# Low halves of four weight tiles computed by POOL instead of DVE, and a new planned price of the transposes

## The chip, the cores and the metric

The kernel runs on one core of a Trainium2 chip. The metric is the device time of one execution in microseconds, the median of several runs. Five engines work side by side: PE (matrix multiplication, with its weight load PEld), DVE (vector), ACT (scalar and activation), POOL (general purpose), and SP, whose queue issues the DMA transfers here.

## The reference

A causal decoder trunk of two layers, for one sequence of 256 tokens of width 1024, all in float32:

```
h = x
for i in range(2):
    mix = moba_attention(h, ...)      if i == 0     # 16 heads of 64
          dilated_attention(h, ...)   if i == 1     # 12 heads of 64, three windows
    h = layer_norm(alpha * h + mix)
    h = layer_norm(alpha * h + square(relu(h @ w_in)) @ w_out)   # 1024 -> 4096 -> 1024
```

Both attentions project to q, k and v, apply rotary embedding to q and k, take a softmax over masked scores, and project back with an output matrix. In the second layer the three groups of four heads have windows 128, 512 and 2048 with steps of 1, 4 and 16, and the groups' results are weighted by their softmax denominators, which comes to one softmax over the three groups together.

## The kernel before

**Numbers in two parts.** To multiply in nearly full float32, every operand is split into a high part, rounded to the matmul's float32r type, and a low part, the difference. A product is then three matmuls: high by high, low by high and high by low. `split` makes the two parts: ACT writes the high one with a copy that rounds (line 337), DVE writes the low one with a subtraction (line 342). For weights, `load_w` takes a `raw` buffer (5 of them, 128x1024 float32, 512 KB), loads a tile into it over SP's queue, and splits it into `whi` and `wlo` (`NSLOT`, 9 of each). 180 tiles of 128x1024 pass this way in one execution.

**Order of the work.** Nothing is issued as it is written. Each step is recorded by `op` with its engine, an assumed duration, and what it reads and writes. `Plan.order` then goes through the steps twice. The first pass runs PE's steps in the order of the program with their assumed durations and gives every step a due time, the latest at which what depends on it is still in time. The second is a list scheduler: for each engine, of the steps that can start first, the one with the earliest due time is taken (DVE may wait a little for a more urgent one). Loads keep their order. The result is a fixed order of instructions for each engine, and the hardware keeps to it, with waits where one engine needs another's result. So an assumed duration is never executed, but changes the order.

**The second layer's attention** follows the string `ORDER1`: three projections `qk-0`, `qk-1`, `qk-2`, each of four weight tiles of 128 output columns, with scores and softmax (`s`), the value projection (`v`), and two output steps (`o`) in between. A projection, `mm_wide`, first multiplies all four tiles' high parts (32 matmuls of 512 columns, the two parts of the input beside each other) and then the four tiles' low parts in order (8 matmuls of 256 columns each). `rotate` applies the rotary embedding on DVE and splits the result into `rhi` and `rlo`, which `score` multiplies. `turned` transposes the softmax result `e` on PE in blocks of 32 columns, 12 blocks to a group of heads in layer 0 and 16 in layer 1, and copies it out as `pt`, two of four parts by DVE and two by ACT in layer 1. Its assumed duration is `0.2 + TURN * len(blocks)`. `pv_dilated` multiplies `pt` by the values and splits the result into `ahi` and `alo`. The output projection reads six weight tiles (`wo1`), the first three for the first output step, the others for the second, each with two token halves and two column halves (`mm_rows`). Then `ln_half` does the LayerNorm: DVE for sums and scaling, POOL for one power instruction of one element per partition (line 756).

**POOL before** does that power instruction eight times, one more at the start, and four small fills. The duration that the planner assumes for elementwise work on POOL is n/480 + 0.17 us for n elements (`tt`), against n/960 + 0.07 on DVE.

Of the kernel before, what the change touches and what calls it, by code (L numbers as in the profile page):

```python
# [10 lines left out]
ALU = mybir.AluOpType  # L11
# [17 lines left out]
NX = (1, 1)  # L29
TAIL = (5, 5, 6, 7)  # L30
NSLOT = 9
TURN = 0.06
DVE1 = (1, 3)
ORDER0 = "qk-0 v-0 qk-1 s-0 o-0 qk-2 s-1 x-0 x-1 o-1 qk-3 s-2 g-0 v-1 s-3 o-2 b-0 o-3"
HEAD1 = "00"
# [54 lines left out]
class Plan:  # L90
# [16 lines left out]
    def op(self, eng, cost, fn, reads=(), writes=(), xfer=0.0, early=0.0, ahead=0.0):  # L107
        o = Op()
        o.n, o.eng, o.cost, o.fn, o.xfer = len(self.ops), eng, cost, fn, xfer
        o.early, o.ahead = early, ahead  # L110
        o.preds, o.succs, o.bufs = set(), [], set()
        for group, is_write in ((reads, False), (writes, True)):
            for item in group:
                b, key = item if isinstance(item, tuple) else (item, None)
                o.bufs.add(b)
                for k, st in b.state.items():
                    if key is None or k is None or k == key:
                        if st[0] is not None:
                            o.preds.add(st[0])
                        if is_write:  # L120
                            o.preds.update(st[1])
                st = b.state.setdefault(key, [None, []])
                if is_write:
                    if key is None:
                        b.state = {None: [o, []]}
                    else:
                        st[0], st[1] = o, []
                else:
                    st[1].append(o)
        o.preds.discard(o)  # L130
        for p in o.preds:
            p.succs.append(o)
        for b in o.bufs:
            b.left += 1
        self.ops.append(o)
        return o
# [141 lines left out]
def tile_trunk(  # L278
# [22 lines left out]
    nc = tc.nc  # L301
    plan = Plan()
    op = plan.op
# [12 lines left out]
    def mk(shape, dt, tag, bufs, space=None):  # L316
        uid[0] += 1
        return plan.buf(Bufs(space or sb, bufs), shape, dt, tag, bufs, f"{tag}_{uid[0]}")

    def psum(tag):  # L320
        return mk([P, 512], F32, tag, 4, ps_pool)

    def f32(ap):
        return ap.bitcast(F32)

    def act(n, aps=0, sbuf=False):
        return n / 1200 + (0.093 if sbuf else 0.055) + 0.093 * aps

    def dve(n, aps=0, fast=False):
        return n / (1920 if fast else 960) + 0.07 + 0.06 * aps  # L330

    def dma(dst, src, reads=(), writes=(), nbytes=0):
        op("SP", ISSUE, lambda: nc.sync.dma_start(dst(), src), reads, writes, xfer=nbytes)  # L333

    def split(n, src, hi, lo, r, whi, wlo, sbuf=False, hi_eng="ACT"):
        if hi_eng == "ACT":
            op("ACT", act(n, sbuf=sbuf), lambda: nc.scalar.activation(hi(), src(), AF.Copy), r, whi)  # L337
        else:
            op("DVE", dve(n), lambda: nc.vector.tensor_copy(hi(), src()), r, whi)
        op(  # L340
            "DVE", dve(n),
            lambda: nc.vector.tensor_tensor(lo(), src(), f32(hi()), op=ALU.subtract), list(r) + list(whi), wlo,  # L342
        )

    def mm(out_ap, lhsT, rhs, start, stop):
# [2 lines left out]
    class W:  # L348
        pass

    def load_w(src, n=1024):
        w = W()
        w.raw = mk([P, 1024], F32, "raw", 5)
        w.hi = mk([P, 1024], F32R, "whi", NSLOT)
        w.lo = mk([P, 1024], F32R, "wlo", NSLOT)
        dma(lambda: w.raw.t[:, :n], src[:, :n], (), [(w.raw, 0)], P * n * 4)
        split(
            n, lambda: w.raw.t[:, :n], lambda: w.hi.t[:, :n], lambda: w.lo.t[:, :n],
            [(w.raw, 0)], [(w.hi, 0)], [(w.lo, 0)], sbuf=True,
        )  # L360
        return w

# [84 lines left out]
    ropes = [const(rope0, [P, 2, S], "ropet")]  # L447
# [127 lines left out]
    def proj_qk(ws):  # L575
        pss = [psum("acc") for _ in ws]
        mm_wide(pss, ws)
        return pss
# [59 lines left out]
    def turned(blocks, r, on_dve=()):  # L638
# [9 lines left out]

        op("PE", 0.2 + TURN * len(blocks), go, list(r) + [ident], pss)
        pt = mk([P, 16, P], F32, "pt", 1)  # L650
# [177 lines left out]
    class Mlp:  # L828
# [3 lines left out]

        def head(self):
            i, nx = self.i, self.nx
            self.ws = [[load_w(win[i][c * 4 + j]) for j in range(4)] for c in range(nx)]
            self.chunks = {c: act_tiles() for c in range(nx)}
            self.half(0)

# [135 lines left out]
    def layer1(between):  # L974
        m1 = late["m1"]
        attn = [act_tiles() for _ in range(2)]

        quads = (((0, 0), (0, 1)), ((0, 2), (1, 0)), ((1, 1), (1, 2)))
        qk, units, seen = {}, {}, [None, None]
        for step, a in (x.split("-") for x in ORDER1.split()):  # L980
            if step == "v":
                v1(int(a[0]), int(a[1]))
                continue
            n = int(a)
            if step == "qk":
                qk[n] = rotate(proj_qk([load_w(wqk1[4 * n + i]) for i in range(4)]), ropes[1])
            elif step == "gb":
                gb = load_gb(2)
            elif step == "s":
                blocks, pss = [], []  # L990
                for u, gi in quads[n]:
                    if u not in units:
                        units[u] = (
                            [[mk([P, 512], F32, "e", 8) for _ in range(2)] for m in range(2)],
                            mk([P, NG, 4], F32, "mx3", 2),
                            mk([P, 8], F32, "sm", 4),
                        )
                    for h in range(2):
                        pss.append(psum("tp"))
                        if gi == 0:  # L1000
                            blocks.append([(halves[m], slice(0, S), m * S) for m in range(2)])
                        else:
                            blocks.append([(halves[m], halves[m], m * P) for m in range(2)])
                score(pss, qk.pop(n), blocks)
                for i, (u, gi) in enumerate(quads[n]):
                    e, st, sm = units[u]
                    w, c0 = (S, 0) if gi == 0 else (P, P + gi * P)
                    g0, seen[u] = seen[u], gi
                    for h in range(2):
                        ps = pss[2 * i + h]  # L1010
                        for m in range(2):
                            r = 2 * h + m
                            mask_min(
                                w, lambda t=e[m][h], c0=c0, w=w: t.t[:, c0 : c0 + w],
                                lambda ps=ps, m=m, w=w: ps.t[:, m * w : (m + 1) * w],
                                lambda m=m, c0=c0, w=w: m1.t[:, m, c0 : c0 + w],
                                lambda st=st, g0=g0, r=r: BIG if g0 is None else st.t[:, g0, r : r + 1],
                                lambda st=st, gi=gi, r=r: st.t[:, gi, r : r + 1],
                                [ps, m1] + ([(st, (g0, r))] if g0 is not None else []), [(e[m][h], gi), (st, (gi, r))],
                            )  # L1020
                    if (n, i) in ((1, 0), (2, 1)):
                        regs = [(e[m][h], 2 * h + m) for h in range(2) for m in range(2)]
                        for t, r in regs:
                            exps(
                                512, lambda t=t: t.t, lambda st=st, r=r, gi=gi: st.t[:, gi, r : r + 1],
                                lambda sm=sm, r=r: sm.t[:, r : r + 1], [t, (st, (gi, r))], [t, (sm, r)],
                            )
                        for t, r in regs:
                            recip(lambda sm=sm, r=r: sm.t[:, r : r + 1], [(sm, r)])
                            scale_by(512, lambda t=t: t.t, lambda sm=sm, r=r: sm.t[:, r : r + 1], [t, (sm, r)], [t])  # L1030
            else:
                e, st, sm = units[n]
                vs, vcs = [], []
                for gi in range(NG):
                    pair = n * NG + gi
                    vs.append(V1[0] if pair < 4 else V1[1])
                    vcs.append(pair * P if pair < 4 else (pair - 4) * P)
                pv_dilated(e, vs, vcs, *attn[n], AHEAD1[n])
        items = [((*attn[j // 3], j % 3), load_w(wo1[j]), j, 6) for j in range(6)]
        out_and_ln(new_acc(), items, TAIL[2], gb, False, between)  # L1040

    mlps = [Mlp(0, False), Mlp(1, True)]
# [119 lines left out]
```

## Time and profile before

| | |
|---|---|
| median of 3 runs | 561.92 us (561.68 to 562.03) |
| profiled execution | 562.14 us, of which the span of instructions 560.3 us |
| granted clock of PE, mean | 0.996 |
| PE busy | 550.7 us (98% of the span), 3459 matmuls |
| DVE busy | 409.9 us (73%) |
| ACT busy | 297.0 us (53%) |
| POOL busy | 8.4 us (1%), 13 instructions |
| DMA | 105.63 MB, mean 189 GB/s |

A row of the timeline or of a group has the engine, the line of the kernel, the operation, `output<-inputs` by tile names, and the shape. Timeline rows begin with start and length in us; a row with x4 is four such instructions in a run, and the bracket at its end tells of idle time before it and of what ended that. In a row of groups, behind the bar, stand the total busy us and the mean ns of one instruction, then the idle us before them and what ended it. Neighbouring instructions of one engine overlap a little in the records, so 4 subtractions of 1.22 us each fill 4.6 us.

### The profile page before, as it was taken

To read this page: it belongs to the slowest core of one execution; us is meant where nothing else is said; L and a number is where in the kernel's file an instruction comes from. 1 tells how busy PE (TensorE), PEld (TensorE's weight loads), DVE (VectorE), ACT (ScalarE), POOL (GpSimd) and SP (SyncE) were. 2 spreads that over 40 slices of the span, in tenths; PEclk is the share of its full clock that TensorE was granted. 3 is DMA by queue.
4 is the path that set the end of the run, shared out by engine and by line. 5 is a ranking of instruction groups with operands and counts; after the bars stand their busy time and mean duration, and the time that the engine had idled before them with its cause. 6 is when DMAs were issued, how large, how long until landed. Compare 5 with 4: busy or idle time off the path is not lost.

```text
span 560.3 us, 8977 instructions
## 1 busy us (share of the span) xinstructions
PE 550.7 (98%) x3459; PEld 467.8 (83%) x3459; DVE 409.9 (73%) x733; ACT 297.0 (53%) x495; POOL 8.4 (1%) x13
## 2 busy tenths in 40 slices
PE   8999999999999999999999999999999999999994
PEld 7888887778888888888888888878888888888884
DVE  6879999797673853855777999998847548557465
ACT  6768866557463555444534547555644554445400
POOL 0000000000000000000000000010000000000000
PEclk9999999999999999999999999999999999999998
DMA  8992345628856755656534742545849566466001
GB/s 309 351 345 81 123 148 178 232 87 318 253 181 269 254 163 185 224 154 223 159 116 156 240 135 101 165 174 199 278 163 303 171 202 225 149 227 194 32 1 75
DMA packets 30138, 105.63 MB, mean 189 GB/s; under 512 B 3344, under 2 KB 4112, under 8 KB 30096
## 3 DMA queue, kind: packets, MB, share of 16 engines
q1 hardware_dynamic: 30096, 105.07, 55.6%
q8 instruction: 27, 0.44, 0.3%
q14 instruction: 15, 0.12, 0.1%
HBM read 104.01 MB, written 1.05 MB: 187 GB/s over the span
## 4 chain that ended last, share of the span: by engine, by line
PE 97%; DMA 1%; DVE 1%; ACT 1%; issue 0%; SPq 0%; DVEq 0%
PE acc L346 58%; PE tp L346 37%; PE tp L632 1%; PE tp L647 1%; DMA raw<-in_xw_dram 1%; DVE tok L547 0%; SPq L333 0%; ACT ta L817 0%; ACT ta L818 0%; ACT whi L337 0%; ACT xs L337 0%; DVE bst L739 0%; DVE tok L540 0%; DVE xs L342 0%; DVEq L1156 0%
## 5 line engine op out<-in xcount | busy, mean ns | idle before, releaser
L342 DVE TENSOR_TENSOR wlo<-raw,whi 128x1024 fp32r<-128x1024 f32 (+2 forms) x185 | 219.7, 1203 | 97.1 <-PE tp L346 53.1
L337 ACT ACTIVATE whi<-raw 128x1024 fp32r<-128x1024 f32 (+2 forms) x184 | 187.4, 1046 | 137.8 <-PE acc L346 60.9
L346 PE MATMUL acc<-whi,ahi 128*128 128x512 f32 (+1 forms) x312 | 121.6, 390 | 0.0
L346 PE MATMUL acc<-wlo,ahi 128*128 128x512 f32 (+1 forms) x312 | 120.9, 388 | 0.0
L346 PE MATMUL tp<-xs,whi 128*128 128x512 f32 x448 | 104.4, 390 | 0.0
L346 PE MATMUL acc<-whi,alo 128*128 128x512 f32 (+1 forms) x312 | 102.9, 387 | 0.0
L346 PEld LDWEIGHTS tp<-xs,whi 128*128 128x128 f32 x448 | 84.0, 188 | 17.4
L346 PEld LDWEIGHTS acc<-whi,alo 128*128 128x128 f32 x312 | 58.6, 188 | 12.1
L346 PEld LDWEIGHTS acc<-whi,ahi 128*128 128x128 f32 x312 | 58.7, 188 | 11.9 <-issue 0.5
L346 PEld LDWEIGHTS acc<-wlo,ahi 128*128 128x128 f32 x312 | 58.7, 188 | 11.2
L346 PE MATMUL acc<-xs,whi 128*128 128x512 f32 (+1 forms) x256 | 58.8, 372 | 0.4 <-ACT xs L337 0.2
L346 PEld LDWEIGHTS tp<-xs,wlo 128*128 128x128 f32 x448 | 55.6, 192 | 1.1
L346 PE MATMUL tp<-xs,wlo 128*128 128x256 f32 x448 | 55.9, 283 | 0.0
L346 PEld LDWEIGHTS acc<-xs,whi 128*128 128x128 f32 x256 | 46.5, 193 | 9.4 <-DVE xs L342 1.2
L540 DVE TENSOR_TENSOR ta<-tp,ta 128x256 f32<-128x256 f32 x56 | 21.8, 418 | 21.8 <-ACT ta L807 21.6
L337 ACT ACTIVATE ahi<-ta 128x256 fp32r<-128x256 f32 x56 | 21.9, 412 | 26.0 <-DVE ta L547 26.0
L807 ACT ACTIVATE ta<-tp 128x256 f32<-128x256 f32 x56 | 21.3, 380 | 25.3 <-PE tp L346 25.3
L346 PE MATMUL acc<-xs,wlo 128*128 128x256 f32 x224 | 33.9, 286 | 0.0
L346 PEld LDWEIGHTS acc<-xs,wlo 128*128 128x128 f32 x224 | 30.5, 194 | 0.7 <-issue 0.2
L346 PE MATMUL acc<-whi,xs 128*128 128x512 f32 (+1 forms) x112 | 28.8, 366 | 0.0
L346 PE MATMUL tp<-whi,xs 128*128 128x512 f32 x80 | 24.8, 397 | 0.3 <-ACT xs L337 0.3
L346 PEld LDWEIGHTS acc<-whi,xs 128*128 128x128 f32 x112 | 19.7, 189 | 3.5 <-DVE wlo L342 0.2
(86 smaller groups left out, 460.9 us busy)
## 6 DMA issues: line engine op xcount, KB each, us to landing
raw<-in_win_dram SPq DMA_DIRECT2D x64, 512.0 KB, 4.5
raw<-in_wout_dram SPq DMA_DIRECT2D x64, 512.0 KB, 4.2
raw<-in_wqk_dram SPq DMA_DIRECT2D x24, 512.0 KB, 4.7
raw<-in_wo_dram SPq DMA_DIRECT2D x14, 512.0 KB, 3.5
raw<-in_wv_dram SPq DMA_DIRECT2D x8, 512.0 KB, 7.8
g<-in_lng_dram SPq DMA_DIRECT2D x4, 512.0 KB, 6.0
b<-in_lnb_dram SPq DMA_DIRECT2D x4, 512.0 KB, 7.3
raw<-in_wv1a_dram SPq DMA_DIRECT2D x4, 512.0 KB, 4.1
```

What stands on the lines that cost most here:

```text
L337: op("ACT", act(n, sbuf=sbuf), lambda: nc.scalar.activation(hi(), src(), AF.Copy), r, whi)
L342: lambda: nc.vector.tensor_tensor(lo(), src(), f32(hi()), op=ALU.subtract), list(r) + list(whi), wlo,
L346: nc.tensor.matmul(out_ap, lhsT, rhs, start=start, stop=stop)
L540: op("DVE", dve(n) + extra, lambda: nc.vector.tensor_tensor(out_ap(), a(), b(), op=alu), r, w)
L632: nc.tensor.transpose(ps.t[:, c : c + P], src(), ident.t)
L647: nc.tensor.transpose(ps.t[:, 32 * i : 32 * i + 32], src()[c, :], ident.t[c, c])
L807: op("ACT", act(S), lambda: nc.scalar.activation(u(), ps.t[:, S:], AF.Copy), [ps], uk)
```

## The change

In the second layer's attention, the low parts of four weight tiles are computed by POOL: tile 3 of the projections `qk-1` and `qk-2`, and tiles 2 and 5 of the output projection. `split` and `load_w` take the engine as an argument. The planner assumes n/480 + 0.17 us for it, 2.30 us for a tile. `PHEAD`, which would name tiles of the MLPs' first chunk, is empty for both layers. `TURN`, the planner's price of a transposed block, goes from 0.06 to 0.071 us, for both layers.

```
-TURN = 0.06
+TURN = 0.071
+PHEAD = ((), ())
+PQK = ((), (3,), (3,))
+PO1 = (2, 5)
...
-    def split(n, src, hi, lo, r, whi, wlo, sbuf=False, hi_eng="ACT"):
+    def split(n, src, hi, lo, r, whi, wlo, sbuf=False, hi_eng="ACT", lo_eng="DVE"):
...
+        eng = nc.vector if lo_eng == "DVE" else nc.gpsimd
         op(
-            "DVE", dve(n),
-            lambda: nc.vector.tensor_tensor(lo(), src(), f32(hi()), op=ALU.subtract), list(r) + list(whi), wlo,
+            lo_eng, dve(n) if lo_eng == "DVE" else n / 480 + 0.17,
+            lambda: eng.tensor_tensor(lo(), src(), f32(hi()), op=ALU.subtract), list(r) + list(whi), wlo,
         )
...
-    def load_w(src, n=1024):
+    def load_w(src, n=1024, lo_eng="DVE"):
...
-            self.ws = [[load_w(win[i][c * 4 + j]) for j in range(4)] for c in range(nx)]
+            self.ws = [[load_w(win[i][c * 4 + j], lo_eng="POOL" if j in PHEAD[i] else "DVE") for j in range(4)] for c in range(nx)]
...
-                qk[n] = rotate(proj_qk([load_w(wqk1[4 * n + i]) for i in range(4)]), ropes[1])
+                qk[n] = rotate(proj_qk([load_w(wqk1[4 * n + i], lo_eng="POOL" if i in PQK[n] else "DVE") for i in range(4)]), ropes[1])
...
-        items = [((*attn[j // 3], j % 3), load_w(wo1[j]), j, 6) for j in range(6)]
+        items = [((*attn[j // 3], j % 3), load_w(wo1[j], lo_eng="POOL" if j in PO1 else "DVE"), j, 6) for j in range(6)]
```

More of the change, by code (lines that the diff above doesn't have):

```diff
@@ L358, in load_w @@
             n, lambda: w.raw.t[:, :n], lambda: w.hi.t[:, :n], lambda: w.lo.t[:, :n],
-            [(w.raw, 0)], [(w.hi, 0)], [(w.lo, 0)], sbuf=True,
+            [(w.raw, 0)], [(w.hi, 0)], [(w.lo, 0)], sbuf=True, lo_eng=lo_eng,
         )
```

## The prediction

> **What bounds the kernel now.** I read the page's totals first, then its chain that ended last, then the busy time by stage, and then the waits of the matmul engine alone.
>
> ```profile
> span 560.3 us, 8977 instructions
> ...
> PE 550.7 (98%) x3459; PEld 467.8 (83%) x3459; DVE 409.9 (73%) x733; ACT 297.0 (53%) x495; POOL 8.4 (1%) x13
> ...
> PE 97%; DMA 1%; DVE 1%; ACT 1%; issue 0%; SPq 0%; DVEq 0%
> ```
>
> PE is busy for 550.7 of 560.3 us, and the chain runs through PE for 97% of the span. All that is not PE adds up to 9.6 us. The question is whether any of it lies where the change acts: the second layer's attention, which on PE's timeline lasts from about 299 to 373 us.
>
> The busy time by stage (PE, PEld, DVE, ACT, POOL, each with its count; then clock, DMA share, GB/s):
>
> ```profile
> 112.60:138.60 26.00, 25.61 (x137) 21.55 (x136) 22.20 (x29) 15.24 (x22) 0.99 (x1) 1.00 0.57 202
> 310.00:373.00 63.00, 63.00 (x602) 53.59 (x601) 59.85 (x135) 36.13 (x63) 0.92 (x1) 1.00 0.53 176
> 373.00:399.00 26.00, 25.64 (x137) 21.52 (x138) 22.27 (x31) 14.93 (x22) 0.92 (x1) 1.00 0.53 182
> 531.00:560.30 29.30, 21.97 (x117) 18.85 (x115) 17.78 (x35) 1.16 (x3) 1.84 (x2) 0.93 0.10 36
> ```
>
> From 310 to 373 us PE is busy 63.00 of 63.00 us at clock 1.00. DVE is nearly full too, with 59.85 us. A second engine so close to full looks like the one to relieve, but it isn't the one that sets the pace: nothing of PE is idle there. PE's idle time lies at the start, in the two transitions from attention to MLP (26.00 - 25.61 = 0.39 us and 26.00 - 25.64 = 0.36 us), and at the end (29.30 - 21.97 = 7.33 us, the last LayerNorm and the store). PE's own waits say the same (for each pair total us, times, longest; the last row is one of ACT's, used further down):
>
> ```profile
> PE tp L346 <- DVE warm L430: 1.2, 1, 1.2
> PE tp L632 <- ACT ta L818: 0.4, 1, 0.4
> PE tp L346 <- ACT xs L337: 0.3, 1, 0.3
> PE acc L346 <- ACT xs L337: 0.2, 1, 0.2
> ...
> ACT whi L337 <- DMA raw<-in_wqk_dram: 2.3, 4, 1.0
> ```
>
> The four PE rows are PE's whole list. The 1.2 us is the start. No matmul of the execution waits for a `wlo` tile, which is what the four moved instructions write. A busy PE can still hide a stall inside a stretched matmul, so I looked at how far apart matmuls start: the 32 matmuls of 512 columns from 310.81 (row below) last 7.44 us, 0.23 each, the pace of all other groups of that shape.
>
> **The change, part by part.** *Four subtractions leave DVE.* Each is one of these:
>
> ```profile
> L342 DVE TENSOR_TENSOR wlo<-raw,whi 128x1024 fp32r<-128x1024 f32 x180 | 216.8, 1220 | 94.6 <-PE tp L346 53.1 <-ACT whi L337 41.3
> ```
>
> 4 x 1.22 = 4.9 us leave DVE, all between 308 and 363 us. They are covered by PE's 63.00 of 63.00 us, so the gain on the path is 0. If PE had been waiting there, it would have been up to 4.9 us.
>
> *Four subtractions arrive on POOL.* No row shows POOL on a large tile. Below, a POOL instruction can't be taken as shorter than DVE's 1.22 us; above, I bound it by when its result is needed. I take 2.3 us, which is the length that the new code itself reckons with (1024/480 + 0.17), as an estimate. The Trainium skill, "GPSIMD Engine Reference", section "Elementwise — side-by-side cycle accounting", gives 4497 ns for 2048 fp32 elements; half of that, 2.25 us, is an estimate from that page and would leave the sum as it is. When ACT has written `whi`, and when PE reads `wlo`:
>
> ```profile
> 309.37 1.05 ACT L337 ACTIVATE whi<-raw 128x1024 fp32r<-128x1024 f32 x1
> 322.40 1.05 ACT L337 ACTIVATE whi<-raw 128x1024 fp32r<-128x1024 f32 x1
> 336.96 2.94 ACT L337 ACTIVATE whi<-raw 128x1024 fp32r<-128x1024 f32 x3
> 356.29 1.99 ACT L337 ACTIVATE whi<-raw 128x1024 fp32r<-128x1024 f32 x2
> ```
>
> ```profile
> 310.81 7.44 PE L346 MATMUL acc<-xs,whi 128*128 128x512 f32 x32
> 318.09 3.99 PE L346 MATMUL acc<-xs,wlo 128*128 128x256 f32 x32
> 340.62 3.02 PE L346 MATMUL acc<-xs,wlo 128*128 128x256 f32 x24
> 358.98 0.50 PE L346 MATMUL acc<-whi,ahi 128*128 128x512 f32 x1
> 363.13 0.50 PE L346 MATMUL acc<-whi,ahi 128*128 128x512 f32 x1
> ```
>
> Counting `whi` tiles along ACT, tile 3 of the second projection (qk-1) is the row at 309.37, done at 310.42; its eight `wlo` matmuls are the last quarter of the row at 318.09, from 318.09 + 3/4 x 3.99 = 321.1: 10.7 us, less 2.3, leaves 8.4 us to spare. Tile 3 of qk-2 is ready at 323.45 and read in the last third of the row at 340.62, from 342.6: 16.9 us to spare. Of the output projection, tile 2 is the last of the three from 336.96, done at 339.90, and first read around 358.98: 16.8 us to spare. Tile 5 is the first of the two from 356.29, done at about 357.3, and read only after the last attention output is there, after 363.13: 3.5 us at least. So even an instruction of 5 us would be in time for each. Cost on the path: 0. Nothing is queued behind these four on POOL but the LayerNorm's power instruction at 370.94, more than 10 us later.
>
> *Loads.* A `raw` buffer is free once both halves of the split have read it. POOL takes its tile as soon as `whi` is there, so the load queue is released earlier or at the same time. ACT's waits for loads are short already (2.3 us in total for this matrix, the last row of the waits above), and behind PE. Cost 0, no gain.
>
> *The transposes' planned price.* `TURN` goes from 0.06 to 0.071 us per block: 0.92 to 1.052 us for 12 blocks (four times in layer 0) and 1.16 to 1.336 for 16 blocks (twice in layer 1). No instruction is added, but due times move by up to 4 x 0.132 + 2 x 0.176 = 0.88 us along the plan, and with them perhaps the order of all engines in both attentions. The chain shows what the transposes last:
>
> ```profile
> 65.56 0.87 PE tp L647 x44
> 339.00 1.12 PE tp L647 x59
> ```
>
> The old price is 0.05 above these rows, the new one 0.18 to 0.22 above; they leave out PE's short pauses on entering and leaving. I bound the effect by the two transitions: best, their 0.39 + 0.36 us vanish; worst, each is doubled: -0.75 to +0.75 us. I take 0, since the chain from the last projection's matmul to the LayerNorm's result and back to PE has no instruction that the change makes shorter.
>
> *Contention between POOL and DVE.* The nearest rows are POOL's 1-element instructions. The first one has no DVE work beside it; the others run beside a pair of DVE instructions that read two tiles of SBUF:
>
> ```profile
> 1.24 0.55 POOL L432 TENSOR_TENSOR warm<-warm,expo 128x1 f32<-128x1 f32 x1 [0.80 <-DVE warm L430]
> 109.24 1.41 DVE L547 SCALAR_TENSOR_TENSOR tok<-tok,mv,g 128x512 f32<-128x512 f32 x2
> 109.41 0.99 POOL L756 TENSOR_TENSOR rstd<-rstd,expo 128x1 f32<-128x1 f32 x1 [107.61 <-DVE rstd L754]
> 370.71 1.41 DVE L547 SCALAR_TENSOR_TENSOR tok<-tok,mv,g 128x512 f32<-128x512 f32 x2
> 370.94 0.92 POOL L756 TENSOR_TENSOR rstd<-rstd,expo 128x1 f32<-128x1 f32 x1 [74.77 <-DVE rstd L754]
> ```
>
> ```profile
> L547 DVE SCALAR_TENSOR_TENSOR tok<-tok,mv,g 128x512 f32<-128x512 f32 x16 | 11.2, 745 | 0.0
> L547 DVE SCALAR_TENSOR_TENSOR tok<-tok,rstd,b 128x512 f32<-128x512 f32 x15 | 10.6, 747 | 0.0
> ```
>
> POOL took 0.55 us alone and 0.92 to 0.99 beside DVE. The first DVE instruction of each pair ends at 109.24 + 0.745 = 109.99 and 371.46; POOL ends at 110.40 and 371.86, both times 0.41 later, though it had started 0.17 and 0.23 after DVE's. So POOL waited for DVE's instruction to end. DVE shows no delay: 745 ns beside POOL, 747 without. For the reverse, POOL holding up DVE, the bounds are 0 and 4 x 2.3 = 9.2 us of DVE time. I take 0 on the path: the only rows show DVE unharmed, and a delay of DVE must first use up its lead on PE.
>
> *Sum:* 0 + 0 + 0 + 0 + 0 on the profiled execution's 562.14 us (span 560.3, and 1.8 around it). That execution lies 0.22 above the median of 561.92, so I predict **561.9 us**. About 0.2%, 1.1 us, is what a measurement of this kernel can tell from no change.
>
> **The rivals.** *B, POOL holds DVE up, slower.* Once a 2.3 us instruction of POOL has its turn, a DVE instruction with two SBUF operands would wait for its end. Where it hurts is where DVE's lead is shortest:
>
> ```profile
> 356.62 0.49 DVE L625 TENSOR_SCALAR e<-e,sm 128x512 f32<-128x512 f32 x1
> 357.02 2.35 DVE L342 TENSOR_TENSOR wlo<-raw,whi 128x1024 fp32r<-128x1024 f32 x2
> 359.29 1.28 DVE L656 COPY pt<-tp 128x512 f32<-128x512 f32 x2
> ```
>
> ```profile
> 361.24 1.96 PE L346 MATMUL tp<-pt,v 128*64 128x256 f32 x24
> ```
>
> The copies end at 360.57 and PE reads them at 361.24: a lead of 0.67 us. Tile 5's subtraction would start at about 357.4, next to the two `wlo` from 357.02, and the copies stand behind these. Held for 2.3 us, PE stalls for 2.3 - 0.67 = 1.6 us: 563.5. It decides once the delay exceeds the lead by 1.1 us, so at a hold of 1.8 us in one such place, or less in two. With a second place of that kind it is 565.1. The other three tiles fall beside the rotary steps; taking them whole too adds at most 4.8. For it: POOL's wait above shows that the two share something. Against it: the new order has one `wlo` less on DVE ahead of each place (1.22 us), and DVE's rows show no harm. The Trainium skill, "SBUF — State Buffer", section "Who interferes with whom", says that a DVE instruction with two SBUF inputs and a GpSimd instruction that reads SBUF share one read interface, and that the one that comes second is blocked until the first is finished. By that rule it is this rival; the trace agrees for POOL behind DVE (0.41 us after), and no row shows DVE behind a long POOL instruction. Chance 0.20.
>
> *C, the schedule gets worse.* The moved due times put a LayerNorm or a softmax step behind a weight tile, and PE waits in either layer. Three new waits like the 0.4 us above make 563.1. For it: PE's order is fixed in advance, so each such lateness counts. Against it: PE's work is the same and always had something ready. Chance 0.04.
>
> *D, faster beyond 0.2%.* Everything that isn't start, end or PE work is 0.39 + 0.36 us, so even with both gone it is 561.9 - 0.75 = 561.2, and the rest of 1.1 us would have to come from the start or the end, where nothing is changed. For it: DVE is 95% full in the attention, and a pause of PE hidden in the modelled ends of its matmuls could go; then some 560.6. Chance 0.08.
>
> *E, the change doesn't do what it says:* POOL far slower than 5 us, so PE waits for tile 5. Within the slower cases, under 0.01.
>
> **How the numbers follow.** No measurable change 0.68, with a range of its own from 561.1 to 562.9; slower 0.20 (B) + 0.04 (C) = 0.24; faster 0.08. The range takes in the same case, the single stall of B (563.5) with a little more for a second short one, and leaves out D's far end and the double stalls: 561.0 to 564.0.
>
> **What would show it.** Right: four POOL rows of 128x1024 around 311, 324, 340 and 357 us; DVE's busy time down by about 4.9 to 405 us; PE's still near 550.7; in 310 to 373 us PE still without idle time; PE's list of waits without `wlo` or `pt`. B shows as DVE rows next to POOL's that last well over 1.22 us, or as gaps in DVE of up to 2.3 us, with PE waiting for `pt`, `rlo` or `e`. C shows as other PE waits in 40 to 110 us. D shows as more than 1.1 us less PE time at the same count of matmuls. The prediction is wrong if PE's idle time outside start and end grows beyond about 2 us, or the span falls below 559.

## The result and the profile after

The changed kernel is slower: 565.33 us (564.45 to 566.8) against 561.97 (561.68 to 562.20), a ratio of 1.0061 with an interval of 1.0049 to 1.0073, or 3.4 us. The prediction was no change at 561.9, in a range up to 564.0. The profiled execution took 566.8 us (span 565.0), the slowest of the four, so its own loss of 4.7 us is more than the typical one; 0.8 us of it is idle time of PE in the first 40 us, far ahead of the four subtractions (38.45 us busy before, 37.69 now).

From the page of the changed kernel:

```profile
span 565.0 us, 8981 instructions
...
PE 552.4 (98%) x3459; PEld 468.6 (83%) x3459; DVE 409.4 (72%) x729; ACT 296.0 (52%) x495; POOL 21.2 (4%) x17
...
PE 93%; DVE 3%; ACT 2%; DMA 1%; issue 1%; SPq 0%; DVEq 0%; ACTq 0%
```

Two things stand out. PE has gone from 97% of the chain to 93%, and DVE and ACT have taken most of what it lost. And DVE is as busy as before, 409.4 against 409.9 us, though four instructions of 1.22 us have left it. PE's busy time grew by 1.7 us at the same 3459 matmuls, so some of them ran slower.

Where PE lost time, by stage and by its waits:

```profile
310.00:373.00 63.00, 61.60 (x588) 52.28 (x587) 56.80 (x126) 35.22 (x61) 12.81 (x4) 0.97 0.53 175
373.00:399.00 26.00, 24.73 (x119) 19.88 (x118) 22.60 (x32) 14.08 (x20) 1.85 (x2) 1.00 0.50 159
```

```profile
PE tp L350 <- ACT xs L340: 1.5, 3, 0.9
PE acc L350 <- DVE ta L544: 1.4, 1, 1.4
PE tp L350 <- DVE warm L434: 1.2, 1, 1.2
PE acc L350 <- ACT xs L340: 0.7, 1, 0.7
PE acc L350 <- DVE xs L346: 0.4, 1, 0.4
```

The attention, full before, now has 63.00 - 61.60 = 1.40 us of idle time, all of it one wait for DVE's `ta` (rotary embedding), and its clock is 0.97 where it was 1.00. The transition to the MLP has 1.27 us idle instead of 0.36, of which 0.9 is a wait for ACT's `xs`. These are two different losses, and the experiments below find a cause for each.

The four subtractions on POOL, and DVE's rows beside the first two:

```profile
310.47 3.31 POOL L346 TENSOR_TENSOR wlo<-raw,whi 128x1024 fp32r<-128x1024 f32 x1 [14.01 <-DVE ta L544]
320.84 2.40 POOL L346 TENSOR_TENSOR wlo<-raw,whi 128x1024 fp32r<-128x1024 f32 x1 [7.07 <-ACT whi L340]
340.07 3.43 POOL L346 TENSOR_TENSOR wlo<-raw,whi 128x1024 fp32r<-128x1024 f32 x1 [16.83 <-ACT whi L340]
353.82 3.68 POOL L346 TENSOR_TENSOR wlo<-raw,whi 128x1024 fp32r<-128x1024 f32 x1 [10.32 <-ACT whi L340]
```

```profile
310.31 1.22 DVE L346 TENSOR_TENSOR wlo<-raw,whi 128x1024 fp32r<-128x1024 f32 x1
311.44 0.75 DVE L544 TENSOR_TENSOR ta<-acc,ta 128x256 f32<-128x256 f32 x2
312.11 4.03 DVE L544 TENSOR_TENSOR ta<-ta,ropet 128x512 f32<-128x512 f32 x4
...
321.41 2.92 DVE L346 TENSOR_TENSOR wlo<-raw,whi 128x1024 fp32r<-128x1024 f32 x1
324.24 0.41 DVE L544 TENSOR_TENSOR ta<-acc,ta 128x256 f32<-128x256 f32 x1
...
340.03 1.22 DVE L346 TENSOR_TENSOR wlo<-raw,whi 128x1024 fp32r<-128x1024 f32 x1
...
352.88 2.35 DVE L346 TENSOR_TENSOR wlo<-raw,whi 128x1024 fp32r<-128x1024 f32 x2
355.15 0.35 DVE L612 CUSTOM_DVE_ANT_0 e<-tp,m,mx 128x128 f32<-128x128 f32 x1
```

Read them together. To say that POOL holds DVE means here that an instruction of DVE has begun in the record but ends later than usual, and only after POOL's. POOL's first starts at 310.47 while a `wlo` of DVE runs until 311.53; it ends at 313.78, 2.25 us after that. The third ends at 343.50, 2.25 after DVE's `wlo` (341.25); the fourth at 357.50, 2.27 after DVE's pair (355.23). So POOL waits for DVE's subtraction and then needs 2.25 us. In those 2.25 us it is DVE that waits. The four rotary products from 312.11 last 4.03 us; in a run further down, where POOL reads nothing, the same four take 2.49. That is 1.54 us of holding: POOL's end at 313.78 lies 1.67 us after the four begin. The `wlo` from 321.41 lasts 2.92 us instead of 1.22, 1.70 us more, POOL's second ending at 323.24. Instructions with one operand in PSUM are not held: `ta<-acc,ta` at 311.44 takes its usual 0.75 for two, and the mask step at 355.15 runs its 0.35 us beside POOL's fourth. In sum 1.54 + 1.70 = 3.24 of the 4.9 us taken off DVE came straight back.

### The profile page after: what moved, and what is told of

It reads as the page before. It is cut to its first block, busy times and chain, and to the rows that moved or that the text cites. A ratio compares the mean times of both kernels' runs of the same rounds, so it can differ in the third digit from the quotient of the medians.

```text
span 565.0 us, 8981 instructions
## 1 busy us (share of the span) xinstructions
PE 552.4 (98%) x3459; PEld 468.6 (83%) x3459; DVE 409.4 (72%) x729; ACT 296.0 (52%) x495; POOL 21.2 (4%) x17
## 4 chain that ended last, share of the span: by engine, by line
PE 93%; DVE 3%; ACT 2%; DMA 1%; issue 1%; SPq 0%; DVEq 0%; ACTq 0%
PE acc L350 55%; PE tp L350 36%; DMA raw<-in_xw_dram 1%; PE tp L651 1%; ACT whi L340 1%; DVE ta L544 1%; DVE wlo L346 1%; PE tp L636 1%; DVE e L612 0%; DVE tok L551 0%; ACT xs L340 0%; SPq L336 0%; ACT ta L821 0%; DVE rlo L346 0%; ACT rhi L340 0%
## 5 line engine op out<-in xcount | busy, mean ns | idle before, releaser
L346 DVE TENSOR_TENSOR wlo<-raw,whi 128x1024 fp32r<-128x1024 f32 (+2 forms) x181 | 216.9, 1212 | 103.9 <-PE tp L350 57.4
L350 PE MATMUL acc<-whi,xs 128*128 128x512 f32 (+1 forms) x112 | 30.4, 376 | 1.4 <-DVE ta L544 1.4
L760 POOL TENSOR_TENSOR rstd<-rstd,expo 128x1 f32<-128x1 f32 x8 | 7.6, 956 | 489.7 <-DVE rstd L758 489.7
```

What stands on the lines that cost most here:

```text
L346: lambda: eng.tensor_tensor(lo(), src(), f32(hi()), op=ALU.subtract), list(r) + list(whi), wlo,
L350: nc.tensor.matmul(out_ap, lhsT, rhs, start=start, stop=stop)
L760: op("POOL", 0.98, lambda: nc.gpsimd.tensor_tensor(rs.t[:, 1:2], rs.t[:, 0:1], expo.t, op=ALU.pow), [(rs, 0), expo], [(rs, 1)])
```

## The experiments

Theory H: POOL's instruction holds DVE's instructions with two operands in SBUF, and that costs the time. Theory O: the new order, which the planner made with the new price and the new engine, costs it. In what follows "the order" is the sequence of instructions on each engine; where a run keeps an order, it is the same instruction for instruction but for what the edit names.

**The new price alone** (`TURN = 0.071` in the kernel before, nothing on POOL).

> The kernel before with the new price of the transposes (0.071) alone; nothing goes to POOL. Theory H (POOL holds DVE up): no instruction of POOL stands beside DVE, so PE has no wait in the second layer's attention, and the time is that of before within 0.5 us, 561.7 to 562.4 (the first layer and the start may bring some 0.3). Theory O (the new order of the instructions costs the time, whoever subtracts): 563.5 to 565.5, with PE waits near 334 or 378 us.

Measured: 562.95 us, ratio 1.0018 (1.0009 to 1.0027). No wait near 334 us, but these three for `xs`, of which the longest, 0.9, is at the transition behind the second layer's attention:

```profile
PE tp L346 <- ACT xs L337: 1.5, 3, 0.9
```

It is the changed kernel's row. So the price alone brings the second loss, about 1 us; the other 2.4 us of the changed kernel need POOL. Neither theory had this split.

**POOL in the order of before** (the planner still reckons with DVE; only the instruction goes elsewhere):

```
+        eng = nc.vector if lo_eng == "DVE" else nc.gpsimd
         op(
             "DVE", dve(n),
-            lambda: nc.vector.tensor_tensor(...), ...
+            lambda: eng.tensor_tensor(...), ...
```

> The order of before for PE, ACT and SP, and for DVE without the four subtractions, which POOL does as soon as it can. Theory H: DVE instructions with two operands in SBUF are held beside POOL's, two or three of them for 1 to 2.25 us each, and POOL takes 2.25 us from the end of DVE's instruction in front; DVE has 4.9 us less to do, so part of it is covered: 562.0 to 564.0. Theory O: no change of order, so no loss, 561.4 to 562.1, and no row of DVE over 1.3 us.

Measured: 562.34 us, ratio 1.0009 (1.0001 to 1.0018). DVE is held as in the changed kernel:

```profile
311.94 4.03 DVE L543 TENSOR_TENSOR ta<-ta,ropet 128x512 f32<-128x512 f32 x4
...
322.20 2.22 DVE L543 TENSOR_TENSOR ta<-ta,ropet 128x512 f32<-128x512 f32 x1
...
349.97 3.11 DVE L345 TENSOR_TENSOR wlo<-raw,whi 128x1024 fp32r<-128x1024 f32 x1
```

4.03 again; 2.22 for a single product, which unheld takes 0.68; and a `wlo` of 3.11 instead of 1.22, beside POOL's fourth subtraction. Together that is 1.54 + 1.54 + 1.89 = 5.0 us of holding, more than the 3.24 of the changed kernel and all of the 4.9 us that were taken off DVE. Yet the time is only about 0.5 us longer here, and PE's wait for `ta` is 0.2 us. Both orders have the hold; what it costs depends on the order around it.

**The changed kernel's order, with POOL hardly reading** (`tiny` in place of the subtraction; the low parts of four tiles are left out):

```
+        def tiny():
+            nc.gpsimd.tensor_tensor(lo()[:, :1], src()[:, :1], f32(hi())[:, :1], op=ALU.subtract)
+            nc.gpsimd.memset(f32(lo())[:, 1:], 0.0)
```

> The order of the changed kernel on all engines, but POOL subtracts only column 0 of each of the four tiles and fills the other 1023 columns with zeros, which reads nothing: the low parts of four tiles are left out. Theory H, with reading as the cause: DVE isn't held, the rows of 2.92 us and 4.03 us go back to about 1.2 and 2.5, PE's wait at 334 us goes; what the order costs alone stays (0.3 in the first layer, up to 0.9 at 378 us): 562.2 to 563.2. Theory O: 564.5 to 565.5 as in the changed kernel.

Measured: 562.56 us, ratio 1.0013 (1.0005 to 1.0022). POOL still writes the tiles at the same places, and DVE isn't held:

```profile
310.49 0.95 POOL L346 MEMSET wlo<- 128x1023 f32 x1
...
320.50 0.95 POOL L346 MEMSET wlo<- 128x1023 f32 x1
```

```profile
311.09 2.49 DVE L549 TENSOR_TENSOR ta<-ta,ropet 128x512 f32<-128x512 f32 x4
...
319.30 1.22 DVE L351 TENSOR_TENSOR wlo<-raw,whi 128x1024 fp32r<-128x1024 f32 x1
...
320.88 0.69 DVE L549 TENSOR_TENSOR ta<-ta,ropet 128x512 f32<-128x512 f32 x1
```

The fill is shorter than the subtraction, so one could think that it holds DVE too, only less. It doesn't: the product at 320.88 has the second fill beside it for most of its length and takes its usual 0.69 us. DVE's busy time is 406.4 us here, 3.0 less than in the changed kernel, about what its two holds come to. With no hold the wait at 334 us is gone, and 2.7 of the 3.4 us with it (ratio 1.0013 instead of 1.0061). The wait for `xs` at the transition, 0.9 us, is still there. By the Trainium skill, "SBUF — State Buffer", section "Who interferes with whom", a DVE instruction with two SBUF inputs contends with a GpSimd instruction that reads SBUF and not with one that only writes it. The trace agrees on both counts (4.03 us for the four products beside the subtraction, 2.49 for the same four and 0.69 for the one beside the fill).

**The changed kernel's order, all on DVE** (`eng = nc.vector`).

> The order of the changed kernel on all engines, with the four subtractions put back on DVE at the place where the plan starts them on POOL. Theory H: no hold, but DVE has 4 x 1.14 us more to do than the plan knows of: 562.2 to 564. Theory O: 565 or more, since to the order's cost DVE's work comes on top.

Measured: 564.01 us, ratio 1.0035 (1.0023 to 1.0047), the upper end of what H expected. PE waits in several small places (0.4 for `ta`, 0.3 for `pt`) and at the transition: DVE seems to have work that this order has no room for; this is argued, not tested. In this order, then, the subtractions cost less on DVE than on POOL (1.0061).

**One pair exchanged on ACT** in the kernel with the new price alone (an instruction is moved in the planner's finished list):

```
         ops = self.order()
+        for o in self.urgent:            # the first xs copy of the second layer's LayerNorm
+            k = ops.index(o)
+            j = max(i for i in range(k) if ops[i].eng == "ACT")
+            ops.insert(k, ops.pop(j))
```

> The kernel with the new price of the transposes alone (562.95 measured), and one pair of neighbours on ACT exchanged: the first xs copy behind the second layer's attention goes before the third of three weight copies (whi) that the plan put ahead of it. If that weight copy, which waits for PE to give back a buffer, is what held xs and so PE for 1.1 us at the transition, the time falls by 0.8 to 1.0, to 561.9 to 562.2, and PE's wait there is 0.2 or less. If the transition's wait has another cause (DVE's LayerNorm steps, or more places of the new order), it stays at 562.7 or above.

Measured: 561.81 us, ratio 0.9992 (0.9984 to 1.0001). ACT's rows without and with the exchange:

```profile
371.52 2.95 ACT L337 ACTIVATE whi<-raw 128x1024 fp32r<-128x1024 f32 x3 [2.79 <-PE acc L346]
374.38 1.06 ACT L337 ACTIVATE xs<-tp 128x512 fp32r<-128x512 f32 x2
```

```profile
371.75 2.01 ACT L343 ACTIVATE whi<-raw 128x1024 fp32r<-128x1024 f32 x2 [2.32 <-PE acc L352]
373.67 0.60 ACT L343 ACTIVATE xs<-tp 128x512 fp32r<-128x512 f32 x1
```

Three weight copies stood in a row, the first of which had to wait for PE to give back a buffer, and `xs`, for which PE itself was about to wait, stood behind all three. Two in front of it are harmless. The ratios, 1.0018 and 0.9992, are about 0.26% apart, and one exchanged neighbour is all that lies between them.

**Only the second hold taken out** (as the filling run, but for tile 3 of `qk-2` alone).

> The order of the changed kernel; POOL does three of its subtractions in full, and of tile 3 of qk-2 only column 0, filling the rest with zeros (its low part is left out). If the holds on DVE cost time only where DVE's lead on PE is used up, and the second one (1.7 us at 321 us) is what uses it up: the row of 4.03 us at 312 stays, that of 2.92 us is gone, PE doesn't wait at 334, and the time is that of the run with all four filled (562.56) or up to 0.6 above it: 562.5 to 563.2. If each hold costs its own length: 564.0 or more.

Measured: 563.14 us (562.42 to 567.55), ratio 1.0035 (1.0015 to 1.0055). The median is what was expected, and so is the profile: the row of 4.03 us is in place, the other `wlo` takes 1.22 us, and PE doesn't wait at 334 us. So the first hold alone doesn't reach PE in this order. But the times scatter, four of the ten lie at 564.9 us or above, and the ratio takes them in. The profiled execution, at 565.5 us, shows part of why it is high:

```profile
345.95 1.06 ACT L340 ACTIVATE whi<-raw 128x1024 fp32r<-128x1024 f32 x1 [2.27 <-DMA raw<-in_wo_dram]
```

```profile
350.11 3.21 POOL L353 TENSOR_TENSOR wlo<-raw,whi 128x1024 fp32r<-128x1024 f32 x1 [9.12 <-ACT whi L340]
```

```profile
349.87 4.54 DVE L353 TENSOR_TENSOR wlo<-raw,whi 128x1024 fp32r<-128x1024 f32 x2
```

ACT waited 2.27 us for a load; in the second profile of the changed kernel (further down) it is 0.49. The steps of ACT, DVE and POOL behind it moved back, not all by the same, and POOL's last subtraction now slid in between two `wlo` of DVE: 4.54 us where the changed kernel has 2.35. PE then waited 0.9 us for `e`. Another 1.1 us of PE's idle time more than before lies in the first 40 us, far ahead of all this. So which engine has the first turn isn't the same in every run of this order, and the cost changes with it; that this makes the other slow executions of this run is not shown, since they have no profile.

**The subtraction in four parts** of 256 columns on POOL.

```
+        def parts():
+            for c in range(0, n, 256):
+                k = slice(c, c + 256)
+                nc.gpsimd.tensor_tensor(lo()[:, k], src()[:, k], f32(hi())[:, k], op=ALU.subtract)
```

> The changed kernel with each of POOL's four subtractions cut into four of 256 columns. If POOL holds DVE only for the length of one instruction of its own, DVE waits for one part (some 0.6 to 0.7 us) at a time and gets its turns in between: no DVE row is held for over 0.8 us, PE's wait at 334 us shrinks below 0.5, and the time is 562.6 to 563.8. If the hold is a matter of the total that POOL reads, the four parts cost what the whole cost, or more by their start-up: 565 to 566.

Measured: 564.17 us, ratio 1.0033 (1.0022 to 1.0045): between the two expectations. The `wlo` that was held for 1.70 us now takes 1.26, but the four rotary products still take 4.11, several short holds in place of one long one, and PE still waits 0.9 us for `ta` instead of 1.4. Three products behind the second subtraction, free in the changed kernel (1.89 us), now take 2.46. Here parts helped the one long DVE instruction, and not the run of short ones.

**The changed kernel again.**

> The changed kernel unaltered, for its spread and a second profile. In the first profile PE waited 1.4 us at 334 us and then ran 3.4 us at half the granted clock. If that slow clock is set off by the wait and not always: times in two groups some 1 to 2 us apart, 564.4 to 565.0 at a mean clock of 0.997 and 565.7 to 566.8 at 0.994, as the four runs so far. If the clock has nothing to do with it: one group, with the same clock.

Measured: 565.38 us (563.64 to 567.42), ratio 1.0065 (1.0044 to 1.0086). The second profile is of an execution of 563.64 us. It has the same holds and the same wait (1.4 us for `ta`), but not the slow clock. The stretch around the wait, in the first and in the second profile:

```profile
332.00:342.00 10.00, 8.60 (x73) 6.85 (x72) 8.86 (x34) 5.32 (x12) 1.93 (x1) 0.83 0.32 108
```

```profile
330.00:340.00 10.00, 8.59 (x110) 6.94 (x109) 9.30 (x37) 6.35 (x13) 1.47 (x1) 1.00 0.33 108
```

The idle time is the same, 1.4 us, but the mean clock of these 10 us is 0.83 in the first and 1.00 in the second: some (1 - 0.83) x 10 = 1.7 us more lost to the one than to the other. The expected two groups by clock did not come out, though. Of the later executions the slowest ones, at 567.2 and 567.4 us, have a mean clock of 0.997. The slow clock is thus one source of the scatter, not the only one. Another is the start: in the first 40 us PE is idle for 1.55 us in the profile before and for 2.31 and 1.66 in the two of the changed kernel.

**Both causes taken out** (POOL filling, and the exchange on ACT).

> Both causes taken out at once: the changed kernel's order with POOL filling (column 0 subtracted, the other low parts of four tiles left out) and the one exchange on ACT at the transition. If the hold of DVE and this one pair of neighbours are all that the change costs, the time is that of before, a ratio of 0.9985 to 1.0005. If a third cause is left in the new order, 1.001 or more.

Measured: 561.94 us, ratio 0.9996 (0.9987 to 1.0005). Nothing that this measurement can tell is left over.

**The exchange alone, in the complete changed kernel.**

> The changed kernel, complete, with the exchange on ACT alone. If the two causes add, it falls from 565.3 by the 0.9 to 1.1 us that the exchange was worth without POOL, to 564.2 to 564.6, and PE's wait at 334 us (1.4 us) stays. If the transition's cost is hidden behind the hold, no change: 565.0 to 565.7.

Measured: 564.85 us, ratio 1.0042 (1.0028 to 1.0056), against 1.0061 and 1.0065 without it. In microseconds that lies between the two expectations, and the intervals overlap, so the times alone don't decide. The profile does: PE's wait for `xs` behind the attention is gone (the longest left is 0.3 us, where it was 0.9), while its wait of 1.4 us for `ta` stays. The two losses are separate.

**Only the two tiles of the output projection, in the order of before.**

> The order of before, and POOL subtracts only tiles 2 and 5 of the output projection; nothing stands beside the rotary steps. DVE has 2.4 us less to do between 349 and 363 us. If DVE doesn't set the pace there, the ratio is 0.999 to 1.0005, with PE's waits as before. If relief of DVE is worth something by itself, it is below 0.998; if POOL's holds cost even here, above 1.001.

Measured: 562.25 us, ratio 0.9997 (0.9989 to 1.0006). The time is that of before, but not because DVE was left in peace:

```profile
348.79 3.10 DVE L345 TENSOR_TENSOR wlo<-raw,whi 128x1024 fp32r<-128x1024 f32 x1
```

POOL's second subtraction starts at 348.43 and holds this `wlo` for 1.9 us, so DVE got back most of the 2.4 us taken off it. The run shows that a hold in this place costs nothing; it doesn't test what relief of DVE is worth.

**The old price, with POOL planned in.**

> The four subtractions on POOL with the old price of the transposes (0.06), planned anew with it: a third order. Holds of DVE beside the rotary steps as in the changed kernel, 1.5 to 2.25 us each; what they cost depends on DVE's lead there: 562.3 (as in the order of before) to 565.3 (as in the changed kernel). A wait at the transition only if the plan puts a third weight copy ahead of xs again.

Measured: 568.53 us, ratio 1.0118 (1.0100 to 1.0136), outside what was expected and the slowest of all. The holds at 312 and 321 us are there with 4.03 and 2.92 us, and in this order a third one falls on the rotary sums of the last projection:

```profile
350.50 2.92 POOL L346 TENSOR_TENSOR wlo<-raw,whi 128x1024 fp32r<-128x1024 f32 x1 [7.26 <-PE acc L350]
```

```profile
350.45 3.51 DVE L544 TENSOR_TENSOR ta<-ta,ta 128x512 f32<-128x512 f32 x2
```

```profile
PE acc L350 <- DVE ta L544: 1.4, 1, 1.4
PE tp L350 <- ACT xs L340: 1.2, 2, 0.9
PE tp L350 <- ACT pt L662: 1.2, 1, 1.2
...
PE tp L350 <- DVE rlo L346: 1.0, 1, 1.0
```

3.51 us where these two take 1.28, and PE then waits for `rlo`, which DVE makes from them, and later for `pt`. The 0.9 us for `xs` is there too, with three weight copies in front of it again, as the expectation allowed. So the new price did not cause the hold, and with POOL in the plan the old one was worse. Nor does the transition's wait need the new price: either change by itself led the planner to that order.

## Why the prediction was wrong, point by point

**What bounds the kernel** was read rightly. PE was full in the attention, and relief of DVE gained nothing: with the four subtractions off DVE, no hold and the pair exchanged, the ratio was 0.9996; with all of them on DVE and the same exchange it was 0.9992.

**POOL's length** was right (2.3 taken, 2.25 to 2.40 measured where it wasn't kept waiting), and so was the conclusion that each `wlo` would be in time: in no run did PE wait for one of the four. The rows behind it were counted one `whi` tile too late, though. In the order of before, POOL's subtractions start at 310.30, 321.41, 339.26 and 349.61 us, not around 311, 324, 340 and 357. Tile 5's `whi` is this row of the profile before, and the pair from 356.29 belongs to the MLP:

```profile
348.09 1.04 ACT L337 ACTIVATE whi<-raw 128x1024 fp32r<-128x1024 f32 x1
```

That leaves more room than was thought, but it moves the place that rival B was worked out for.

**The contention term, taken as 0 on the path, is the step that failed.** It rested on rows with POOL instructions of one element. These show that POOL waits for DVE, as it does here. That DVE showed no delay, 745 against 747 ns, told little of a long one: POOL's work on one element ended 0.41 us after DVE's instruction, and that of a 128x1024 tile ends 2.25 us after it. The wait of POOL in the same rows was evidence that the two take turns. The measured term is 3.24 us of DVE time in the changed kernel, inside the stated bounds of 0 to 9.2. On the path, from the kernel with the hold and without (ratios 1.0061 and 1.0013), it is 0.48%, or 2.7 us.

**The lead of DVE on PE** was the second half of that step. That a delay must first use it up was right, as the order of before shows, where 5.0 us of holding cost 0.5. Rival B (chance 0.20) had the mechanism right and the place wrong. It put the stall at tile 5 and the copies of `pt`, where DVE's lead was 0.67 us, and had for the rotary steps only a bound of 4.8 us. But in the order of before tile 5's subtraction starts at 349.61 us, not at 357.4; it held a `wlo` there, and PE waited for no `pt`. In the changed kernel it ran beside mask steps, which read PSUM and aren't held. The stall came at the first rotary step of `qk-2`, behind the two holds beside the rotary steps of `qk-0` and `qk-1`. How the delay reached PE is in the changed kernel's rows:

```profile
334.03 1.06 ACT L340 ACTIVATE whi<-raw 128x1024 fp32r<-128x1024 f32 x1 [2.41 <-DVE wlo L346]
334.99 0.37 ACT L558 ACTIVATE ta<-acc 128x256 f32<-128x256 f32 x1
```

```profile
335.39 0.42 DVE L544 TENSOR_TENSOR ta<-acc,ta 128x256 f32<-128x256 f32 x1 [0.40 <-ACT ta L558]
```

```profile
331.38 1.11 PE L350 MATMUL acc<-xs,wlo 128*128 128x256 f32 x8
...
335.87 0.50 PE L350 MATMUL acc<-whi,xs 128*128 128x512 f32 x1 [1.40 <-DVE ta L544]
```

A weight copy on ACT waited for a late `wlo` of DVE; the copy out of the accumulator, whose last matmuls ended at 332.49 (the first PE row), stood behind it; DVE's last step on that accumulator then took 0.42 us, and only after it did PE write into it. In the order of before ACT has no such weight copy in that place, and the two holds there, 3.1 us, cost PE a wait of 0.2 us. With the copy in its place and no hold (POOL filling) PE didn't wait for `ta` at all. So it takes the hold and the order together; that it is this neighbour in the order is argued from the rows, since no run exchanged it alone.

**The price of the transposes, taken as 0 in bounds of 0.75 us** around it, was wrong too. Alone it measured 0.18% against before and 0.26% against the kernel with one exchanged pair: 1.0 to 1.5 us. The bound was made by doubling the transitions' idle time; but an order can bring in waits that weren't there, and they have no row in the profile of before. Rival C named this (a LayerNorm step behind a weight tile) and had a chance of 0.04.

**The loads** were rightly of no account in the plan, but perhaps not in the scatter: in one profile POOL's turn had moved where ACT had waited 2.27 us for a load.

**The bounds.** A gain was rightly ruled out. The prediction's own sign of being wrong, over about 2 us of idle time of PE outside start and end, came true: 1.40 us in the attention and 0.91 more at the transition. The top, 564.0, came from one short stall. With both mechanisms at their worked-out prices, 1.6 us for B and 1.2 for C, it would have been 564.7. That this comes near 565.33 is luck: the stall was in another place and 1.4 us long, and C's three new waits were one of 0.9 us. Of the 2.7 us that the hold costs, PE's wait explains 1.4. The slow clock behind it adds some 1.7 us in one profile and nothing in the other; what makes up the rest in the typical execution stays open.

## What to carry to other kernels

An engine that is nearly full is worth relieving only if the pacing engine waits for it; here PE was full, and the best outcome was no change. Before an elementwise instruction goes to POOL, look at what DVE does beside it: in these runs, with two operands in SBUF on both sides the two took turns, each for a whole instruction, so POOL's length counted against DVE; a DVE instruction with one operand in PSUM, or a POOL instruction that only writes, was not touched. What such holds cost, from nothing to 2.7 us here, is a matter of who stands behind it. And where a planner makes the order, a changed price is a change of its own: compare the orders, and test the price by itself.

## What the runs showed of the hardware

The hold was expected as a possibility, its regularity was not: POOL's subtraction of 128x1024 ended 2.25, 2.25 and 2.27 us after DVE's in front of it. Which of the two went first changed with the moment at which POOL came: 0.94 us after the start of the first of two `wlo` it had to wait for both (353.82 in the changed kernel), 0.24 us after it POOL went in front of the second (350.11 in the run with one fill).

After a wait of only 1.4 us PE's granted clock fell to about half for 3.3 us in one profile of the changed kernel. It stayed at 1.00 in three other profiles with the same wait: the second one of the changed kernel, and those of the runs with the exchange in it and with the old price. The slow stretch of the first:

```profile
336.40:339.70 3.30, 3.30 (x9) 2.52 (x8) 3.30 (x20) 3.30 (x9) 0.00 (x0) 0.52 0.54 176
```

The Trainium skill, "TensorE: Matmul & The Clock Gate", section "Why this matters for your kernels", has as its rule of practice no idle gaps of over about 3 us between bursts of matmuls. This profile differs: its gap is half as long. In front of it PE had 2.0 us of small score matmuls; whether these count as little work for the clock was not tried, and that the wait set off the slow clock is not shown.
